# Prompt attention scores: the queries' lo parts multiplied with the 64 rows of the keys' hi, one component on each half of the rows

## The chip, the cores and the metric

The kernel runs on one core of one Trainium2 chip. The metric is device time in microseconds (us) of one execution, the median over runs. A core has a matrix engine (TensorE, PE in the profile; its weight loads are listed apart as PEld), a vector engine (VectorE, DVE), a scalar engine (ScalarE, ACT), GpSimd (POOL) and a queue engine that issues transfers (SyncE, SP). SBUF is the working memory with 128 rows (partitions); TensorE accumulates into PSUM.

## What is computed

One step of a decoder layer: a combined input projection, a state-space group, differential attention, an output projection and a gated feed-forward part with a short convolution. The change touches the prompt's attention scores only:

```python
def _scores(q, k):            # c: two components of 64 numbers per head
    return jnp.einsum('bthcd,bshcd->bhcts', q, k).astype(jnp.float32) * (QK_DIM ** -0.5)

def _diff_weights(s, lam):
    p = jax.nn.softmax(s, axis=-1)
    return p[:, :, 0] - lam * p[:, :, 1]

# bounds: 16 meta tokens, then blocks of 128 queries; L = 2064, 4 heads
for s0, e0 in bounds:
    s = _scores(q[:, s0:e0], k[:, :e0])
    mask = jnp.arange(e0)[None, :] <= jnp.arange(s0, e0)[:, None]
    w = _diff_weights(jnp.where(mask, s, NEG), lam)
    outs.append(jnp.einsum('bhts,bshe->bthe', w.astype(v.dtype), v[:, :e0]))
```

## The kernel before

Float32 products are made of two reduced-precision parts: a number x is split into hi (what the matrix engine's faster 32-bit format, fp32r, holds) and lo = x - hi.

**Where the parts come from.** `put_k` and `put_q` take one 128-token tile of the projection, normalise it per head, transpose it and split it. The keys go to scratch memory `KST[h, c]`, 128 rows deep: rows 0 to 63 the hi part of component c, rows 64 to 127 its lo part. The queries go to `QST[s, h, c]`, s = 0 for hi and 1 for lo, 64 rows each.

**The scores.** `attend` walks over two halves of the sequence, four heads in each, and in each of these over groups `g` of two 128-query tiles. `load_queries` fetches a group's queries into `qs` and writes each part twice, into rows 0 to 63 and into rows 64 to 127, so that one matmul over 128 rows multiplies one part of the query with hi and lo of the key. `attend_scores` makes one 128-query tile: for each component c, and for each piece z of at most 512 keys, a PSUM buffer `S` (a pool of four) gets qhi x (khi + klo) (L468), qlo x (khi + klo) (L469) and, where the piece touches the diagonal, a causal mask by a bfloat16 matmul (L472). DVE then takes the row maximum (L474) and ACT the exponential (L475), which frees the `S` buffer. After all pieces of a component come small steps that join the pieces (L480 to L484); after both components POOL and DVE form the weighted difference (L505, L507). `attend_values` transposes the weights (`tpw`, L530) and multiplies them with the values (`O`, L537).

**What sets the order.** The program is written tile by tile, but a scheduler in the compiler decides the order in which each engine's instructions stand, from priorities and its own estimate of times; an engine then runs its list in that order. While the attention runs, the scheduler puts matmuls of two later stages between it: the state-space half of the output projection (`out_ssm`, tile `po`, operands `sa`) and the first tiles of the attention half (`out_attention`, tile `po`, operands `oa`). These are written with `mm3` (L80, L81, L82: hi x hi, hi x lo, lo x hi). Later stages named below: `sample_attention` (tiles `tps`, `os`, `att`) and the feed-forward's up projection (tile `g`, again `mm3`).

Of the kernel before, what the change touches and what calls it, by code (L numbers as in the profile page):

```python
# [10 lines left out]
F32 = mybir.dt.float32  # L11
# [3 lines left out]
AF = mybir.ActivationFunctionType  # L15
ALU = mybir.AluOpType
AX = mybir.AxisListType
# [3 lines left out]
P = 128  # L21
D = 1024
KT = D // P
NM = 16
TP = 2064
# [35 lines left out]
class Step:  # L61
# [278 lines left out]
    def put_k(self, wp, pt, pj, t, n):  # L340
        nc, o = self.nc, self.o
        kg = self.heads_norm(wp, pj, n, self.gk)
        m = min(n, TP - t * P)
        kp = o["k_prompt"][0, 0].rearrange("t h d -> t (h d)")
        nc.sync.dma_start(out=kp[t * P : t * P + m], in_=kg[:m])
        if m < n:
            nc.sync.dma_start(out=o["k_sample"][0].rearrange("s t h d -> (s t) (h d)"), in_=kg[m:n])
        hi, lo = self.heads_T(wp, pt, kg, n, self.kTs)
        for c in range(2):
            for x, at in ((hi, 0), (lo, 64)):  # L350
                nc.sync.dma_start(
                    out=self.KST[:, c, at : at + 64, t * P : t * P + m].rearrange("h d t -> d h t"),
                    in_=x[c * 64 : c * 64 + 64, :, :m].bitcast(F32))
# [76 lines left out]
    def load_queries(self, qs, h, q0, q1):  # L430

        for dup in range(2):
            for s in range(2):
                self.nc.sync.dma_start(out=qs[dup * 64 : dup * 64 + 64, s, :, : q1 - q0].bitcast(F32),
                                       in_=self.QST[s, h, :, :, q0:q1].rearrange("c d t -> d c t"))

    def attend_queries(self, grp, wp):
        h, g = grp["h"], grp["g"]
# [6 lines left out]
    def attend_scores(self, grp, qi, wp, vp, ps):  # L445

        nc = self.nc
        qs, kt = grp["qs"], grp["head"]["kt"]
        M = P if qi else NM
        W = NM + P * qi  # L450
        Wall = NM + P * grp["nb"]
        qa = (NM + P * (qi - 1) if qi else 0) - grp["q0"]
        Z = P - NM
        diag = W - M
        nz = -(-W // 512)
        cuts = [W * z // nz // 2 * 2 for z in range(nz + 1)]
        pw, sums, fs = [], [], []
        for c in range(2):

            p = vp.tile([P, P - NM + TP], F32, name="p", tag="p", bufs=7)  # L460
            nms = wp.tile([P, 5], F32, name="nms", tag="nms", bufs=12)
            sms = wp.tile([P, 5], F32, name="sms", tag="sms", bufs=12)
            for z in range(nz):
                x, y = cuts[z], cuts[z + 1]
                S = ps.tile([P, 512], F32, name="S", tag="S", bufs=4)
                dst = S[:M, : y - x]
                masked = y > diag
                nc.tensor.matmul(dst, lhsT=qs[:, 0, c, qa : qa + M], rhs=kt[c][:, x:y], start=True, stop=False)  # L468
                nc.tensor.matmul(dst, lhsT=qs[:, 1, c, qa : qa + M], rhs=kt[c][:, x:y], start=False, stop=not masked)  # L469
                if masked:  # L470
                    lo_ = max(diag, x)
                    nc.tensor.matmul(dst[:, lo_ - x : y - x], lhsT=self.identB[:, :M],  # L472
                                     rhs=self.maskB[:, lo_ - diag : y - diag], start=False, stop=True)
                nc.vector.tensor_reduce(out=nms[:M, z : z + 1], in_=dst, axis=AX.X, op=ALU.max, negate=True)  # L474
                nc.scalar.activation(p[:M, Z + x : Z + y], dst, AF.Exp, bias=nms[:M, z : z + 1], accum_out=sms[:M, z : z + 1])  # L475
            sm, f = sms[:, 0:1], None
            if nz > 1:

                nm = wp.tile([P, 1], F32, name="nm", tag="nm", bufs=12)
                nc.vector.tensor_reduce(out=nm[:M], in_=nms[:M, :nz], axis=AX.X, op=ALU.min)  # L480
                f = wp.tile([P, 5], F32, name="f", tag="f", bufs=12)
                nc.scalar.activation(f[:M, :nz], nms[:M, :nz], AF.Exp, scale=-1.0, bias=nm[:M])
                sm = wp.tile([P, 1], F32, name="sm", tag="sm", bufs=12)
                nc.vector.scalar_tensor_tensor(out=sms[:M, :nz], in0=f[:M, :nz], scalar=1.0, in1=sms[:M, :nz],  # L484
                                               op0=ALU.mult, op1=ALU.mult, accum_out=sm[:M])
            pw.append(p)
            sums.append(sm)
            fs.append(f)

        cf = wp.tile([P, 1], F32, name="cf", tag="cf", bufs=8)  # L490
        c0 = wp.tile([P, 1], F32, name="c0", tag="c0", bufs=8)
        nc.vector.reciprocal(cf[:M], sums[1][:M])
        nc.gpsimd.tensor_tensor(out=c0[:M], in0=sums[0][:M], in1=self.nlam[:M], op=ALU.mult)
        nc.gpsimd.tensor_tensor(out=cf[:M], in0=cf[:M], in1=c0[:M], op=ALU.mult)
        w = pw[0]
        nc.gpsimd.memset(w[:M, 0:Z], 0.0)
        if nz == 1:
            nc.vector.scalar_tensor_tensor(out=w[:M, Z : Z + W], in0=pw[1][:M, Z : Z + W], scalar=cf[:M],
                                           in1=w[:M, Z : Z + W], op0=ALU.mult, op1=ALU.add)
        else:  # L500
            g = wp.tile([P, 5], F32, name="g", tag="gf", bufs=8)
            nc.gpsimd.tensor_tensor(out=g[:M, :nz], in0=fs[1][:M, :nz], in1=cf[:M].to_broadcast([M, nz]), op=ALU.mult)
            for z in range(nz):
                x = slice(Z + cuts[z], Z + cuts[z + 1])
                nc.gpsimd.tensor_tensor(out=pw[1][:M, x], in0=pw[1][:M, x],  # L505
                                        in1=g[:M, z : z + 1].to_broadcast([M, x.stop - x.start]), op=ALU.mult)
                nc.vector.scalar_tensor_tensor(out=w[:M, x], in0=w[:M, x], scalar=fs[0][:M, z : z + 1], in1=pw[1][:M, x],  # L507
                                               op0=ALU.mult, op1=ALU.add)
        if W < Wall:
            nc.gpsimd.memset(w[:M, Z + W : Z + Wall], 0.0)  # L510
        z = qi - 9 * grp["head"]["half"]
        nc.gpsimd.tensor_tensor(out=grp["head"]["e2"][:M, z : z + 1], in0=sums[0][:M], in1=sums[0][:M], op=ALU.mult)
        return w
# [1226 lines left out]
```

## Time and profile before

| | |
|---|---|
| median of 3 runs | 2938.07 us (2932.61 to 2941.27) |
| profiled execution | 2936.48 us, its span 2934.7 us |
| mean granted TensorE clock | 0.973 |
| PE busy | 2750.9 us (94%), 14916 matmuls |
| DVE / ACT / POOL busy | 2225.7 (76%) / 1403.3 (48%) / 1000.8 us (34%) |
| score matmuls | 360 at L468, 360 at L469, 136 masks at L472, from 642.8 us to 1186 us |

How to read it: a matmul's start is recorded, its end is modelled, and matmuls overlap in the pipeline, so the time that one costs is read from its start to the next one's start, not from its listed duration. A busy PE is therefore not a PE without waste; an idle PE has certainly waited. In the listings "128\*128 128x412" is a weight tile of 128 rows and 128 columns through which 412 columns pass; the number ahead of the star is the count of rows that take part. The granted clock is given as a share of 2.4 GHz; 0.5 would be the lower of the clock's two levels.

### The profile page before, as it was taken

How to read it: one execution, taken by the hardware profiler on the slowest of the kernel's cores; microseconds unless marked ns; L12 is line 12 of the kernel's file. 1: busy time of each engine (PE TensorE's matmuls, PEld its weight loads, DVE VectorE, ACT ScalarE, POOL GpSimd, SP SyncE). 2: the span in 40 equal slices, each digit the busy share in tenths (PEclk: the TensorE clock that was granted, in tenths of full speed). 3: DMA queues.
4: the chain of work that ended last, by engine and by line, in shares of the span. 5: the costliest groups of instructions: out<-in, count | busy, mean ns of one | idle time of the engine just before them, and what ended most of it. 6: DMA issues, size and time to landing. Idle time of an engine off the chain costs nothing.

```text
span 2934.7 us, 43647 instructions
## 1 busy us (share of the span) xinstructions
PE 2750.9 (94%) x14916; PEld 2364.0 (81%) x14916; DVE 2225.7 (76%) x4317; ACT 1403.3 (48%) x2859; POOL 1000.8 (34%) x1381
## 2 busy tenths in 40 slices
PE   6989989979999899787999999999999998999999
PEld 6966667867887777676998998988999997778776
DVE  6748876757678898557898878898889994675566
ACT  3323223545556666335566556665565562222234
POOL 4525442115445576564243432343214441000000
PEclk9999999989999999999999999999999999999999
DMA  7876776977864332587455546454454447676554
GB/s 224 255 194 149 205 216 168 236 216 195 230 182 141 116 113 83 166 266 228 156 161 186 160 145 213 145 181 159 133 168 130 127 125 290 216 245 195 178 190 132
DMA packets 452553, 529.73 MB, mean 181 GB/s; under 512 B 91546, under 2 KB 353578, under 8 KB 451305
## 3 DMA queue, kind: packets, MB, share of 16 engines
q1 hardware_dynamic: 360584, 385.75, 45.0%
q10 hardware_dynamic: 72848, 72.79, 7.5%
q0 software_dynamic: 18896, 68.39, 7.4%
q8 instruction: 118, 1.93, 0.3%
q14 instruction: 107, 0.87, 0.1%
HBM read 390.49 MB, written 135.14 MB: 179 GB/s over the span
## 4 chain that ended last, share of the span: by engine, by line
PE 55%; DVE 9%; DMA 8%; POOL 2%; issue 2%; ACT 2%; SPq 0%; ACTq 0%; POOLq 0%; DVEq 0%
PE g L80 8%; PE g L81 8%; PE g L82 8%; PE pq L80 4%; PE pq L81 4%; PE pq L82 4%; PE O L537 3%; DVE p L507 2%; DMA ot<-RR 2%; PE po L80 1%; DMA oraw<-in_w_out_dram 1%; DMA dt<-MT 1%; PE po L81 1%; PE po L82 1%; PE tps L632 1%
## 5 line engine op out<-in xcount | busy, mean ns | idle before, releaser
L80 PE MATMUL g<-xb,uw 128*128 128x384 f32 (+1 forms) x1848 | 594.0, 324 | 8.8 <-DVE A L1408 4.8
L81 PE MATMUL g<-xb,uw 128*128 128x384 f32 (+1 forms) x1848 | 595.8, 323 | 1.2 <-DVE xb L69 1.2
L82 PE MATMUL g<-xb,uw 128*128 128x384 f32 (+1 forms) x1848 | 584.7, 322 | 0.4 <-DVE uw L69 0.4
L80 PEld LDWEIGHTS g<-xb,uw 128*128 128x128 f32 x1848 | 346.8, 188 | 19.3 <-DVE A L1408 5.3
L81 PEld LDWEIGHTS g<-xb,uw 128*128 128x128 f32 x1848 | 347.9, 188 | 9.1 <-issue 2.3
L82 PEld LDWEIGHTS g<-xb,uw 128*128 128x128 f32 x1848 | 346.1, 188 | 7.0 <-issue 1.2
L475 ACT ACTIVATE p<-S,nms 128x484 f32<-128x484 f32 (+11 forms) x360 | 210.1, 589 | 157.6 <-DVE nms L474 136.0
L80 PE MATMUL pq<-dw,da 128*128 128x512 f32 x616 | 245.9, 401 | 19.6 <-ACT da L68 11.8
L69 DVE TENSOR_TENSOR uw<-uraw,uw 128x512 fp32r<-128x512 f32 x330 | 239.5, 734 | 26.7 <-ACT uw L68 24.7
L68 ACT ACTIVATE uw<-uraw 128x512 fp32r<-128x512 f32 x330 | 201.0, 625 | 114.6 <-PE g L82 77.2
L81 PE MATMUL pq<-dw,da 128*128 128x512 f32 x616 | 245.5, 399 | 0.0
L82 PE MATMUL pq<-dw,da 128*128 128x512 f32 x616 | 236.9, 398 | 0.0
L474 DVE TENSOR_REDUCE nms<-S 128x1 f32<-128x484 f32 (+11 forms) x360 | 190.9, 554 | 40.9 <-PE S L469 27.4
L68 ACT ACTIVATE da<-dt 128x1024 fp32r<-128x1024 f32 x66 | 69.8, 1058 | 249.4 <-PE pq L82 149.3
L95 POOL TENSOR_TENSOR rs_y<-rs_v,half 128x8 f32<-128x8 f32 (+4 forms) x77 | 105.8, 1377 | 243.9 <-DVE rs_v L90 225.9
L80 PE MATMUL pj<-wh,x 128*128 128x512 f32 (+1 forms) x408 | 170.6, 419 | 8.1 <-ACT wh L74 5.7
L81 PE MATMUL pj<-wl,x 128*128 128x512 f32 (+1 forms) x408 | 170.3, 417 | 2.7 <-DVE wl L75 2.6
L82 PE MATMUL pj<-wh,x 128*128 128x512 f32 (+1 forms) x408 | 169.6, 416 | 0.0
L468 PE MATMUL S<-kt,qs 128*128 128x484 f32 (+11 forms) x360 | 145.7, 407 | 23.3 <-ACT p L475 13.5
L1311 POOL TENSOR_TENSOR uraw<-uraw 128x512 f32<-128x512 f32 x66 | 108.0, 1637 | 160.6 <-DVE s L1309 112.4
L80 PEld LDWEIGHTS pq<-dw,da 128*128 128x128 f32 x616 | 117.2, 190 | 50.5 <-ACT da L68 12.7
L505 POOL TENSOR_TENSOR p<-p,g 128x412 f32<-128x412 f32 (+13 forms) x164 | 156.5, 983 | 3.4
(423 smaller groups left out, 6895.7 us busy)
## 6 DMA issues: line engine op xcount, KB each, us to landing
dt<-MT SPq DMA_DIRECT2D x99, 512.0 KB
uraw<-in_w_gate_dram SPq DMA_DIRECT2D x66, 512.0 KB
uraw<-in_w_up_dram SPq DMA_DIRECT2D x66, 512.0 KB
raw<-in_w_in_dram SPq DMA_DIRECT2D x80, 256.0 KB
MT<-z ACTq DMA_DIRECT2D x44, 384.0 KB
dT<-in_w_down_dram SPq DMA_DIRECT2D x66, 256.0 KB
qs<-QST SPq DMA_DIRECT2D x128, 128.0 KB
draw<-in_w_down_dram SPq DMA_DIRECT2D x55, 256.0 KB
```

Of the source, the lines that this page charges most:

```text
L68: nc.scalar.activation(hi, src, AF.Copy)
L69: nc.vector.tensor_tensor(out=lo, in0=src, in1=hi.bitcast(F32), op=ALU.subtract)
L80: mm(out, lhsT=lh, rhs=rh, start=start, stop=False, skip_group_check=goes_on)
L81: mm(out, lhsT=lh, rhs=rl, start=False, stop=False, skip_group_check=goes_on)
L82: mm(out, lhsT=ll, rhs=rh, start=False, stop=stop, skip_group_check=goes_on)
L95: nc.gpsimd.tensor_tensor(out=y, in0=v, in1=e, op=ALU.pow)
L468: nc.tensor.matmul(dst, lhsT=qs[:, 0, c, qa : qa + M], rhs=kt[c][:, x:y], start=True, stop=False)
L474: nc.vector.tensor_reduce(out=nms[:M, z : z + 1], in_=dst, axis=AX.X, op=ALU.max, negate=True)
L475: nc.scalar.activation(p[:M, Z + x : Z + y], dst, AF.Exp, bias=nms[:M, z : z + 1], accum_out=sms[:M, z : z + 1])
L505: nc.gpsimd.tensor_tensor(out=pw[1][:M, x], in0=pw[1][:M, x], in1=g[:M, z : z + 1].to_broadcast([M, x.stop - x.start]), op=ALU.mult)
L537: nc.tensor.matmul(O[:, :N], lhsT=v, rhs=tw[:, m - a, :N], start=(m == 0), stop=(m == nb))
L1311: gp.tensor_tensor(out=a21, in0=a11, in1=a21, op=ALU.subtract)
```

## The change

Three edits.

- `put_k`: for component 1 the halves of `KST` swap places, so that khi lies in rows 0 to 63 for component 0 and in rows 64 to 127 for component 1.
- `load_queries`: hi is still written twice for both components; of lo only component 0 goes to rows 0 to 63 and component 1 to rows 64 to 127. The number of transfers stays (144), half of them carry half the bytes.
- `attend_scores`: the loop over components moves inside the loop over pieces. For one piece both components get the 128-row pass with qhi and their mask; then come two matmuls with qlo that read 64 rows only, component 0 on rows 0 to 63, component 1 on rows 64 to 127; then maximum and exponential of both. The product qlo x klo is no longer formed.

```diff
         for c in range(2):
-            for x, at in ((hi, 0), (lo, 64)):
+
+            for x, at in ((hi, 64 * c), (lo, 64 - 64 * c)):
                 nc.sync.dma_start(
                     out=self.KST[:, c, at : at + 64, t * P : t * P + m].rearrange("h d t -> d h t"),
...
         for dup in range(2):
-            for s in range(2):
-                self.nc.sync.dma_start(out=qs[dup * 64 : dup * 64 + 64, s, :, : q1 - q0].bitcast(F32),
-                                       in_=self.QST[s, h, :, :, q0:q1].rearrange("c d t -> d c t"))
+            rows = slice(dup * 64, dup * 64 + 64)
+            self.nc.sync.dma_start(out=qs[rows, 0, :, : q1 - q0].bitcast(F32),
+                                   in_=self.QST[0, h, :, :, q0:q1].rearrange("c d t -> d c t"))
+            self.nc.sync.dma_start(out=qs[rows, 1, dup, : q1 - q0].bitcast(F32), in_=self.QST[1, h, dup, :, q0:q1])
...
-            for z in range(nz):
-                x, y = cuts[z], cuts[z + 1]
+        for z in range(nz):
+            x, y = cuts[z], cuts[z + 1]
+            masked = y > diag
+            dst = []
+            for c in range(2):
                 S = ps.tile([P, 512], F32, name="S", tag="S", bufs=4)
-                dst = S[:M, : y - x]
-                masked = y > diag
-                nc.tensor.matmul(dst, lhsT=qs[:, 0, c, qa : qa + M], rhs=kt[c][:, x:y], start=True, stop=False)
-                nc.tensor.matmul(dst, lhsT=qs[:, 1, c, qa : qa + M], rhs=kt[c][:, x:y], start=False, stop=not masked)
+                dst.append(S[:M, : y - x])
+                nc.tensor.matmul(dst[c], lhsT=qs[:, 0, c, qa : qa + M], rhs=kt[c][:, x:y], start=True, stop=False)
                 if masked:
                     lo_ = max(diag, x)
-                    nc.tensor.matmul(dst[:, lo_ - x : y - x], lhsT=self.identB[:, :M],
-                                     rhs=self.maskB[:, lo_ - diag : y - diag], start=False, stop=True)
-                nc.vector.tensor_reduce(out=nms[:M, z : z + 1], in_=dst, axis=AX.X, op=ALU.max, negate=True)
-                nc.scalar.activation(p[:M, Z + x : Z + y], dst, AF.Exp, bias=nms[:M, z : z + 1], accum_out=sms[:M, z : z + 1])
+                    nc.tensor.matmul(dst[c][:, lo_ - x : y - x], lhsT=self.identB[:, :M],
+                                     rhs=self.maskB[:, lo_ - diag : y - diag], start=False, stop=False)
+
+            for c in range(2):
+                r = slice(64 * c, 64 * c + 64)
+                nc.tensor.matmul(dst[c], lhsT=qs[r, 1, c, qa : qa + M], rhs=kt[c][r, x:y], start=False, stop=True)
+            for c in range(2):
+                p, nms, sms = stat[c]
+                nc.vector.tensor_reduce(out=nms[:M, z : z + 1], in_=dst[c], axis=AX.X, op=ALU.max, negate=True)
+                nc.scalar.activation(p[:M, Z + x : Z + y], dst[c], AF.Exp, bias=nms[:M, z : z + 1], accum_out=sms[:M, z : z + 1])
```

In the changed file the hi pass stands at L472, the mask at L475, the lo pass at L480, the transposes of the weights at L541 and the value matmuls at L548. The scheduler orders the new program again. PE's list, one head of the second half, a tile of 452-column pieces, before (the number behind a tile's name tells buffers apart; kt_9062 holds component 0 of the keys, kt_9064 component 1):

```order
L530 MATMUL tpw_9430<-ident_63,p_9163 128x128 x4
L530 MATMUL tpw_9441<-ident_63,p_9085 128x128 x4
L468 MATMUL S_9353<-kt_9062,qs_9262 128x452
L469 MATMUL S_9353<-kt_9062,qs_9262 128x452
L468 MATMUL S_9358<-kt_9062,qs_9262 128x452
L469 MATMUL S_9358<-kt_9062,qs_9262 128x452
L468 MATMUL S_9363<-kt_9062,qs_9262 128x452
L469 MATMUL S_9363<-kt_9062,qs_9262 128x452
L472 LDWEIGHTS identB_68
L472 MATMUL S_9363<-maskB_76,identB_68 128x128
L468 MATMUL S_9378<-kt_9064,qs_9262 128x452
L469 MATMUL S_9378<-kt_9064,qs_9262 128x452
```

The same tile's pieces in PE's list of the changed kernel:

```order
L472 MATMUL S_9361<-kt_9062,qs_9262 128x452
L480 MATMUL S_9361<-kt_9062,qs_9262 128x452
L541 MATMUL tpw_9447<-ident_63,p_9163 128x128 x3
L472 MATMUL S_9363<-kt_9064,qs_9262 128x452
L480 MATMUL S_9363<-kt_9064,qs_9262 128x452
L541 MATMUL tpw_9447<-ident_63,p_9163 128x128
L541 MATMUL tpw_9458<-ident_63,p_9085 128x128 x3
L472 MATMUL S_9371<-kt_9062,qs_9262 128x452
L480 MATMUL S_9371<-kt_9062,qs_9262 128x452
```

The components alternate now, but the lo pass of component 0 (L480, kt_9062) stands right behind its own hi pass, ahead of component 1's hi pass; the two lo passes of a piece are apart, with 128-row matmuls between them.

PE's list of the changed kernel at a piece with the diagonal, one head further on:

```order
L472 MATMUL S_11159<-kt_10875,qs_11118 128x420
L475 LDWEIGHTS identB_68
L475 MATMUL S_11159<-maskB_76,identB_68 128x128
L480 MATMUL S_11159<-kt_10875,qs_11118 128x420
L472 MATMUL S_11162<-kt_10877,qs_11118 128x420
L475 LDWEIGHTS identB_68
L475 MATMUL S_11162<-maskB_76,identB_68 128x128
L480 MATMUL S_11162<-kt_10877,qs_11118 128x420
L472 MATMUL S_11207<-kt_10875,qs_11118 128x452
```

Here the mask has moved from behind the lo pass to between the hi pass and the lo pass of its component; before, it was followed by another buffer's work.

## Rows read from the trace of the kernel before

**Rows 1.** The page's first part: busy time, share of the span, instructions

```profile
PE 2750.9 (94%) x14916; PEld 2364.0 (81%) x14916; DVE 2225.7 (76%) x4317; ACT 1403.3 (48%) x2859; POOL 1000.8 (34%) x1381
```

**Rows 2.** Busy us of each engine by stretch: start:end, length, engines, clock, DMA share, GB/s

```profile
640.00:700.00 60.00, 49.13 (x236) 37.84 (x237) 42.08 (x120) 34.59 (x111) 23.76 (x69) 0.85 0.87 244
700.00:900.00 200.00, 200.00 (x1103) 168.81 (x1101) 147.91 (x407) 104.95 (x350) 92.47 (x238) 0.98 0.67 190
900.00:1200.00 300.00, 276.54 (x1485) 224.69 (x1484) 262.03 (x625) 190.19 (x552) 180.43 (x293) 0.98 0.37 110
```

**Rows 3.** Chain of waits, its shares by line, 700 to 900 us, then 900 to 1200

```profile
by line: PE O L537 20.7%; PE po L80 13.5%; PE po L82 12.9%; PE po L81 12.8%; PE S L468 12.2%; PE tpw L530 10.9%; PE S L469 10.7%; PE SS L552 3.8%; PE S L472 2.4%; PE tpr L564 0.2%
...
by line: DVE p L507 16.4%; DVE nms L474 12.3%; PE O L537 9.7%; DMA ot<-RR 6.1%; POOL p L505 4.7%; issue 4.6%; PE tpw L530 3.7%; PE S L468 3.5%; DMA oraw<-in_w_out_dram 3.4%; DVE wT L534 3.2%; PE S L469 2.8%; DVE sms L484 2.6%; PE po L80 2.4
```

**Rows 4.** The lo pass L469 alone by stretch: PE, PEld, clock, DMA share, GB/s

```profile
640.00:700.00 60.00, 14.38 (x40) 8.86 (x40) 0.85 0.87 244
700.00:900.00 200.00, 42.15 (x128) 24.45 (x128) 0.98 0.67 190
900.00:1200.00 300.00, 69.36 (x193) 36.73 (x192) 0.98 0.37 110
```

**Rows 5.** PE's timeline in the scores: start us, listed duration, instruction

```profile
1023.82 0.37 PE L469 MATMUL S<-kt,qs 128*128 128x484 f32 x1
1024.04 0.23 PE L472 MATMUL S<-maskB,identB 128*128 128x128 bf16 x1
1024.08 0.47 PE L81 MATMUL po<-owl,oa 128*128 128x512 f32 x1
1024.39 0.35 PE L468 MATMUL S<-kt,qs 128*128 128x412 f32 x1
1024.58 0.35 PE L469 MATMUL S<-kt,qs 128*128 128x412 f32 x1
```

**Rows 6.** PE's timeline, a 32-row matmul between 128-row ones (sample attention)

```profile
1530.98 0.34 PE L82 MATMUL g<-xb,uw 128*128 128x384 f32 x1
1531.24 0.44 PE L680 MATMUL os<-vnh,swT 32*64 32x512 f32 x1
1531.62 0.44 PE L80 MATMUL g<-xb,uw 128*128 128x384 f32 x1
1531.90 0.33 PE L81 MATMUL g<-xb,uw 128*128 128x384 f32 x1
```

**Rows 7.** PEld's timeline at the same place, idle time before in brackets

```profile
1531.24 0.13 PEld L680 LDWEIGHTS os<-vnh,swT 32*64 32x64 f32 x1 [0.25 <-ACT vh L686]
1531.62 0.19 PEld L80 LDWEIGHTS g<-xb,uw 128*128 128x128 f32 x1 [0.24 <-issue]
```

**Rows 8.** PE's timeline, sixteen 64-row transposes between 128-row matmuls

```profile
1496.34 0.33 PE L82 MATMUL g<-xb,uw 128*128 128x384 f32 x1
1496.51 0.34 PE L81 MATMUL g<-xb,uw 128*128 128x384 f32 x1
1496.78 1.21 PE L672 MATMUL tps<-ident,Ss 64*128 64x64 f32 x16
1497.92 0.45 PE L82 MATMUL g<-xb,uw 128*128 128x384 f32 x1
1498.21 0.34 PE L80 MATMUL g<-xb,uw 128*128 128x384 f32 x1
```

**Rows 9.** PE's timeline, 64-row float32 matmuls, then 128-row ones of 512 columns

```profile
1538.73 0.34 PE L81 MATMUL g<-xb,uw 128*128 128x384 f32 x1
1539.00 1.04 PE L699 MATMUL att<-om,sel 64*32 64x512 f32 x2
1539.97 0.45 PE L680 MATMUL os<-vh,swT 128*64 128x512 f32 x1
1540.26 0.39 PE L681 MATMUL os<-vl,swT 128*64 128x512 f32 x1
1540.48 0.39 PE L680 MATMUL os<-vh,swT 128*64 128x512 f32 x1
```

More of the change, by code (lines that the diff above doesn't have):

```diff
@@ L457, in attend_scores @@
         pw, sums, fs = [], [], []
+        stat = []
         for c in range(2):
-            p = vp.tile([P, P - NM + TP], F32, name="p", tag="p", bufs=7)
-            nms = wp.tile([P, 5], F32, name="nms", tag="nms", bufs=12)
-            sms = wp.tile([P, 5], F32, name="sms", tag="sms", bufs=12)
-            for z in range(nz):
-                x, y = cuts[z], cuts[z + 1]
+            stat.append((vp.tile([P, P - NM + TP], F32, name="p", tag="p", bufs=7),
+                         wp.tile([P, 5], F32, name="nms", tag="nms", bufs=12), wp.tile([P, 5], F32, name="sms", tag="sms", bufs=12)))
@@ L476, in attend_scores @@
+        for c in range(2):
+            p, nms, sms = stat[c]
             sm, f = sms[:, 0:1], None
```

## The prediction

> **What bounds the kernel now.** The page's first part says which engine to suspect: TensorE is busy for 94% of the span, DVE for 76% [rows 1]. That is an average, so the table of busy times by stretch comes next, over the part in which scores are made [rows 2]. It shows three regimes. From 640 to 700 us TensorE is busy for 49.1 of 60 us: the stage starts and waits for its first data. From 700 to 900 us it is busy for all 200 us, DVE for 148: here TensorE alone is the limit. From 900 to 1200 us TensorE is idle for 300 - 276.5 = 23.5 us and DVE is busy for 262 of 300. The chain of waits agrees [rows 3]: from 700 to 900 us every line of it is TensorE's (the scores' two passes 12.2% and 10.7%), from 900 to 1200 us DVE's weighted difference and row maximum lead, and TensorE's lines follow. So time added to TensorE's list is paid whole between 700 and 900 us, and after 900 us once its 23.5 us of waiting are used up.
>
> **Costs of a matmul, from starts to next starts.** A lo pass of 484 columns takes 0.22 us, a hi pass of 412 columns 0.19 us [rows 5]. The cost goes with the columns; nothing in these rows lets fewer rows make it shorter. The question is what it costs to stand a 64-row matmul among 128-row ones. Before, the scores use 128 rows throughout; other stages have such neighbours.
>
> The nearest row in kind is a 32-row matmul of the same number format, alone between 128-row ones [rows 6]. From the start of the 128-row matmul ahead of it (1530.98) to the second start behind it (1531.90) pass 0.92 us. Undisturbed the three would take 0.17 + 0.22 + 0.17 = 0.56 us (384 columns 0.17 in rows 8, 512 columns 0.22 in rows 9). So going in and out costs about **0.35 us**: 0.09 ahead of it, 0.16 in it, 0.11 behind it. The weight loads show why [rows 7]: both PEld rows stand behind 0.25 and 0.24 us of idle, so in neither case were the weights loaded while the matmul ahead was running.
>
> With 64 rows the same edges are there: at the transposes 1496.51 to 1496.78 is 0.27 instead of 0.17, and 1497.92 to 1498.21 is 0.29 instead of 0.17, together 0.22 us [rows 8]; at the float32 matmuls 0.27 instead of 0.17 and 0.29 instead of 0.22, together **0.17 us** [rows 9]. What these lose inside can't be told apart from their own work, so 0.17 is the lower end. I take 0.35, the row that has the format of the new matmuls and its cost in full; its edges (0.09 and 0.11) are those of the 64-row rows.
>
> The Trainium skill has a rule for this: "TensorEngine Tiling (Array Packing)", section Key Properties, says that changing the tiling mode, and not just the tile, drains the engine. That speaks against this change, and rows 6 and 7 agree with 0.35 us for a way in and out.
>
> **Part 1, the lo pass on 64 rows.** It removes no columns: 360 lo matmuls before, 360 after, of the same widths. What decides is how they stand in TensorE's list. The text of the change puts the two components' lo matmuls side by side; the scheduler does not. In the order shown above the lo pass of component 0 follows its own hi pass, and 128-row matmuls stand between the two lo passes of a piece. Counted over the whole list, the 360 lo matmuls form 341 runs: 323 of one, 17 of two, one of three. Only 18 of 180 pairs touch. So there are **341 ways in and out**: 341 x 0.35 = 119 us of TensorE time.
>
> **Part 2, the masks.** Before, 93 of the 136 masks are followed by a matmul of the fp32r format (a hi pass or `po`), and that one takes 0.31 instead of 0.22 us, for its weights come late (1024.08 to 1024.39, rows 5). After, 134 masks stand between hi and lo of their own buffer, where the lo pass waits anyway. That gives back up to 93 x 0.09 = 8 us. Sum on TensorE: 119 - 8 = 111 us.
>
> **Part 3, what costs nothing.** DVE's, ACT's and POOL's instructions are the same in number and size. Half of the query transfers carry half the bytes; the DMA engines are busy for 37% to 67% of the time after 700 us [rows 2], so smaller transfers free nothing that was short. The swapped halves of the keys' scratch move nothing in time. The two components now end together, so their joining steps bunch up; the work on other tiles covers it, and if that cover fails it can cost at most the idle time that I count as used up below (23.5 us).
>
> **Where the 111 us land.** The lo passes lie 40, 128 and 193 to the three stretches [rows 4], so 11%, 35% and 54%: 12, 39 and 60 us. From 640 to 700 us there are 10.9 us of idle time; between 0 and 12 us, I take 6. From 700 to 900 us nothing hides it: 39. From 900 to 1200 us the waiting of 23.5 us goes first: 60 - 23.5 = 36. Sum: 6 + 39 + 36 = **81 us**. On the profiled execution's 2936.5 us that is 3017.5; the median of the runs is 1.6 us above that execution, so 3019 us. Behind the stage nothing gives the time back: the same `po` matmuls stand inside it before and after, 552 of them.
>
> Ends: with 0.17 us for a run the sum is 341 x 0.17 - 8 = 50 us, of which the first stretch's 6 vanish, 17 are paid and 27 - 23.5 = 4 remain: 21 us, 2959 us. With 0.35 and no idle time used up, because the waits after 900 us stay as long as they are, all 111 us are paid: 3049 us.
>
> **Rivals.**
> *A. The 64-row fp32r matmul costs nothing extra*, the loss in rows 6 being one of 32 rows, that in rows 8 and 9 one of other formats. Then only the masks' 8 us remain, half of them in the stretch with waiting: about 2930 to 2934 us, no change that can be told (0.3%, 8.8 us, is about what a measurement of this kernel can tell). Against it: three kinds of matmul show the same edges. It decides from a price of 0.1 us for a run: 341 x 0.1 - 8 = 26 us, of which 9 are paid between 700 and 900 us and the rest lies in idle time. Chance 0.07.
> *B. The pairs run at the same time*, which ends on the other side. Two matmuls on different halves of the rows would take the time of one, 0.19 us less for a pair, 34 us for 180 pairs, if they touched. They touch at 18 places: 3 us. With A's price that is 2938 - 8 - 3 = 2927 us, just faster. No row before shows two matmuls side by side in different rows. Chance 0.03. (The Trainium skill, "TensorE: Matmul & The Clock Gate", Part 3 on row and column tiling, has them start about 4 ns apart; by it a pair would save what is said here, but only where it touches, and no run here shows it yet.)
> *C. The clock falls.* TensorE's granted clock is 0.98 from 700 us on and was 0.85 in the stretch in which it waits most [rows 2]. If the new gaps bring the 500 us behind to 0.85 as well, streaming grows by 0.98/0.85 - 1 = 15%, at most 76 us more: up to 3095 us. Against it: behind the edges of rows 9 the second matmul passes 512 columns in 0.22 us, which is the higher level of the clock (2.4 GHz), and no row shows an edge that brings it down. Chance 0.05.
>
> **How the numbers follow.** The forecast has 0.85, A 0.07, B 0.03, C 0.05. Predicted is 3019 us; the range is the forecast's own, 2959 to 3049, which leaves out A, B and C, 0.15 in all. Slower by over 0.3%: 0.85 + 0.05 = 0.90. Within 0.3%: 0.07. Faster: 0.03.
>
> **What would show it.** In the profile after, from a 128-row matmul's start to the start of the lo pass behind it some 0.09 us more than its columns take, the lo pass itself 0.16 more, the next one 0.11 more; PEld idle ahead of almost every lo pass's weights and ahead of the next. The stretch of the scores longer by some 80 us, with TensorE's waits for ACT and DVE in it shorter, and everything behind it shifted and not longer. Wrong: a lo pass that starts without a gap (A); two that start within a few ns, at many places (B); a granted clock under 0.95 in the scores (C); the added time lying behind the scores, which would mean that the scheduler's new order costs something I did not see.

## The result: slower by 3.2%, close to the forecast

| | before | changed |
|---|---|---|
| median of the runs beside each other | 2939.67 us | 3034.82 us |
| ratio | | 1.0322, 95% interval 1.0298 to 1.0347 |
| span of the profiled execution | 2934.7 us | 3030.0 us |

The forecast was 81 us more (3019 us, range 2959 to 3049); it became 95 us more.

Where the time lies is read from the same views as before. First the page's first part of the changed kernel (busy us, share, instructions); it answers to [rows 1]:

```profile
PE 2860.4 (94%) x14916; PEld 2378.9 (79%) x14916; DVE 2220.8 (73%) x4317; ACT 1411.3 (47%) x2859; POOL 994.5 (33%) x1381
```

The same number of matmuls, 110 us more of TensorE. The table by stretch (start:end, length, PE, PEld, DVE, ACT, POOL, granted clock, DMA share, GB/s), against [rows 2]:

```profile
640.00:700.00 60.00, 52.11 (x181) 33.72 (x182) 34.69 (x98) 30.62 (x91) 20.24 (x57) 0.72 0.73 208
700.00:900.00 200.00, 200.00 (x920) 145.72 (x918) 117.39 (x348) 92.96 (x304) 72.35 (x209) 0.97 0.53 159
900.00:1200.00 300.00, 299.05 (x1328) 205.90 (x1328) 227.07 (x527) 166.96 (x479) 146.66 (x255) 0.99 0.35 105
```

In the 200 us in which TensorE was the limit it now makes 920 matmuls instead of 1103. From 900 to 1200 us it is idle for 1 us instead of 23.5: the stretch in which DVE led has become TensorE's as well. The chain of waits, shares by line, 700 to 900 us and 900 to 1200 us, says the same against [rows 3]; the lo pass (L480) has 17.3% and 21.2% of it, before (L469) 10.7% and 2.8%:

```profile
by line: PE O L548 19.3%; PE S L480 17.3%; PE po L80 13.5%; PE S L472 12.5%; PE po L82 11.2%; PE po L81 10.6%; PE tpw L541 10.2%; PE SS L563 2.8%; PE S L475 2.3%; PE tpr L575 0.2%
...
by line: PE O L548 23.5%; PE S L480 21.2%; PE S L472 16.0%; PE tpw L541 13.1%; PE po L80 6.6%; PE po L82 6.3%; PE po L81 6.3%; PE SS L563 1.6%; DMA oraw<-in_w_out_dram 1.2%; PE S L475 1.1%; PE tp L179 1.0%; issue 0.6%; DVE nms L483 0.4%; DV
```

The cost of one lo pass can be read from TensorE's timeline of the changed kernel (start us, listed duration, instruction):

```profile
865.94 0.40 PE L81 MATMUL po<-owl,sa 128*128 128x512 f32 x1
866.18 0.39 PE L82 MATMUL po<-owh,sa 128*128 128x512 f32 x1
866.41 0.38 PE L472 MATMUL S<-kt,qs 128*128 128x484 f32 x1
866.72 0.48 PE L480 MATMUL S<-kt,qs 64*128 64x484 f32 x1
867.12 0.50 PE L80 MATMUL po<-owh,sa 128*128 128x512 f32 x1
867.46 0.39 PE L81 MATMUL po<-owl,sa 128*128 128x512 f32 x1
867.69 0.38 PE L472 MATMUL S<-kt,qs 128*128 128x484 f32 x1
```

From each start to the next one: the hi pass ahead of the lo pass takes 0.31 us where 484 columns take 0.22 [rows 5], 0.09 more; the lo pass 0.40, 0.18 more; the matmul behind it 0.34 where 512 columns take 0.23 (867.46 to 867.69), 0.11 more. Together 0.38 us at this place. Over the whole trace a lone lo pass takes 0.21 us more than its columns would at 2.4 GHz (median of 321 without idle time behind them), in the kernel before 0.02 us more (median of 339). The weight loads at the same place show that neither the lo pass's weights nor those behind it are loaded ahead (idle time before in brackets), as in [rows 7]:

```profile
866.18 0.19 PEld L472 LDWEIGHTS S<-kt,qs 128*128 128x128 f32 x1
866.71 0.18 PEld L480 LDWEIGHTS S<-kt,qs 64*128 64x128 f32 x1 [0.35 <-issue]
867.12 0.19 PEld L80 LDWEIGHTS po<-owh,sa 128*128 128x128 f32 x1 [0.23 <-issue]
867.23 0.19 PEld L81 LDWEIGHTS po<-owl,sa 128*128 128x128 f32 x1
```

Scores and value products began at 642.8 us and ended at 1212 us before; in the changed kernel they run from 644.9 to 1297 us. So 83 of the 95 us are in that stage, 2 us ahead of it, 10 us behind it, as the two profiled executions have it.

### The profile page after: what moved, and what is told of

The parts are those of the page before. It is cut to its first block, busy times and chain, and to the rows that moved or that the text cites. A ratio compares the mean times of both kernels' runs of the same rounds, so it can differ in the third digit from the quotient of the medians.

```text
span 3030.0 us, 43593 instructions
## 1 busy us (share of the span) xinstructions
PE 2860.4 (94%) x14916; PEld 2378.9 (79%) x14916; DVE 2220.8 (73%) x4317; ACT 1411.3 (47%) x2859; POOL 994.5 (33%) x1381
## 4 chain that ended last, share of the span: by engine, by line
PE 60%; DVE 8%; DMA 6%; issue 2%; POOL 2%; ACT 1%; SPq 0%; ACTq 0%; POOLq 0%; DVEq 0%
PE g L82 7%; PE g L80 7%; PE g L81 7%; PE O L548 5%; PE S L480 4%; PE pq L80 4%; PE pq L81 4%; PE pq L82 4%; PE S L472 3%; PE tpw L541 2%; DVE uw L69 2%; PE po L80 2%; PE po L82 2%; PE po L81 2%; PE tps L643 1%
## 5 line engine op out<-in xcount | busy, mean ns | idle before, releaser
L483 DVE TENSOR_REDUCE nms<-S 128x1 f32<-128x484 f32 (+11 forms) x360 | 197.2, 561 | 110.3 <-PE S L480 107.3
L472 PE MATMUL S<-kt,qs 128*128 128x484 f32 (+11 forms) x360 | 153.6, 434 | 9.2 <-DMA qs<-QST 7.0
L480 PE MATMUL S<-kt,qs 64*128 64x484 f32 (+11 forms) x360 | 155.5, 456 | 0.0
```

What stands on the lines that cost most here:

```text
L472: nc.tensor.matmul(dst[c], lhsT=qs[:, 0, c, qa : qa + M], rhs=kt[c][:, x:y], start=True, stop=False)
L480: nc.tensor.matmul(dst[c], lhsT=qs[r, 1, c, qa : qa + M], rhs=kt[c][r, x:y], start=False, stop=True)
L483: nc.vector.tensor_reduce(out=nms[:M, z : z + 1], in_=dst[c], axis=AX.X, op=ALU.max, negate=True)
```

## The experiments

The theory (H): a 64-row matmul among 128-row ones costs about 0.4 us for the way in and out, and the scheduler leaves 341 such ways. The rival (O): the new order, with the components interleaved and their joining steps late, is what costs. A second question was whether the pairs would pay if they really stood back to back.

The times below are medians, and the kernel before has been run beside each group of experiments. Its executions spread over 27 us (2919.69 to 2946.38 in the first group). The recorded ratios of the experiments with four executions stand on a base 4 to 10 us above the median of all the executions of the kernel before (3035.40 / 1.0322 = 2941 against 2932), so differences of 10 us between experiments carry no argument here.

**The order alone.** The changed kernel's loops, lo pass on 128 rows:

```diff
-                r = slice(64 * c, 64 * c + 64)
-                nc.tensor.matmul(dst[c], lhsT=qs[r, 1, c, qa : qa + M], rhs=kt[c][r, x:y], start=False, stop=True)
+                nc.tensor.matmul(dst[c], lhsT=qs[:, 1, c, qa : qa + M], rhs=kt[c][:, x:y], start=False, stop=True)
```

with the old `put_k` and `load_queries`. 

> The changed kernel's loops, but the lo pass reads all 128 rows as before, with the old layout of the keys and the old loads of the queries; the lo product of both lo parts is formed again. Theory H (the way in and out of a 64-row matmul costs 0.40 us, 341 times): no 64-row matmul is left among the scores, so the time falls back to the kernel before, 2930 to 2950 us; the lo pass is listed as 128*128 and starts without a gap. Rival O (the new order of the components, with their joining steps bunched at the end of a tile, starves the engines): most of the 95 us stays, 3010 to 3035 us.

Measured: 2922.76 us against 2932.03 us of the kernel before, ratio 0.9968 (0.9946 to 0.9991). That is under the 2930 to 2950 us that H gave. The rival falls: the order costs nothing, it is 9 us better. Against these loops the 64 rows cost 3034.8 - 2922.8 = 112 us; taken against the kernel before that ran beside each of them it is 95 + 9 = 104 us. The order alone also goes back to the old layout and the old loads; in the changed kernel TensorE waits for neither, since it has 1 us of idle time from 700 to 1200 us. The table of the order alone from 900 to 1200 us looks like that of before, TensorE waiting for 23 us again:

```profile
900.00:1200.00 300.00, 277.20 (x1503) 226.41 (x1501) 259.86 (x611) 182.24 (x534) 183.47 (x291) 0.99 0.40 120
```

**The rows alone.** The loops of the kernel before, lo pass on 64 rows, new layout and loads:

```diff
-                nc.tensor.matmul(dst, lhsT=qs[:, 1, c, qa : qa + M], rhs=kt[c][:, x:y], start=False, stop=not masked)
+                r = slice(64 * c, 64 * c + 64)
+                nc.tensor.matmul(dst, lhsT=qs[r, 1, c, qa : qa + M], rhs=kt[c][r, x:y], start=False, stop=not masked)
```

> The loops of the kernel before, but the lo pass reads 64 rows, with the new layout of the keys and the new loads. Its list has 359 runs of lo matmuls instead of 341. Theory H: 359 x 0.40 = 144 us on TensorE, less some 25 to 37 us of idle time that is used up: 3040 to 3065 us, slower than the changed kernel. Rival O: within 15 us of the kernel before, 2925 to 2955 us.

Measured: 3035.40 us, ratio 1.0322 (1.0287 to 1.0357). Far from the rival's 2955 us; 5 us under the lower end of what H gave, so the 18 more ways in and out than in the changed kernel do not show. Nor is it a comparison of the ways alone, for the granted clock is 0.96 here where the changed kernel has 0.99. TensorE has no idle time left from 900 to 1200 us:

```profile
900.00:1200.00 300.00, 300.00 (x1293) 202.76 (x1294) 223.88 (x522) 163.97 (x469) 138.88 (x247) 0.96 0.34 101
```

**Half of the heads.** The changed kernel, heads 2 and 3 with 128-row lo passes:

```diff
-                r = slice(64 * c, 64 * c + 64)
+                r = slice(64 * c, 64 * c + 64) if grp["h"] < 2 else slice(0, P)
```

with lo of both components loaded into all rows for these heads. 

> The changed kernel, but heads 2 and 3 load both components' lo into all 128 rows and make the lo pass on 128 rows; heads 0 and 1 keep the 64-row lo pass. About 171 runs of 64-row matmuls are left of 341. Theory H (a price for each way in and out): 171 x 0.40 = 68 us on TensorE above the same loops without 64-row matmuls (2923 us), less the idle time that goes first: 2960 to 2985 us, about half of the way to the changed kernel. A rival by which the first few 64-row matmuls already cost most of it (a lasting effect such as a lower clock): 3010 us or more.

Measured: 2975.68 us against 2933.92 us, ratio 1.0129 (1.0096 to 1.0162). That is 53 us above the loops without 64-row matmuls (2922.76 us, from another group of runs), 47% of the whole 112 us with half of the ways (171): about half, as H said, and not the 3010 us of a lasting effect. Of the 23 us of idle time from 900 to 1200 us, 8.4 us are left:

```profile
900.00:1200.00 300.00, 291.59 (x1472) 222.24 (x1471) 254.38 (x598) 185.42 (x541) 170.42 (x282) 1.00 0.36 111
```

**Pairs that really touch, and their control.** The changed kernel with both components' scores in one PSUM tile of two banks, so that both hi passes get their buffer at once:

```diff
+            S = ps.tile([P, 2, 512], F32, name="S", tag="S", bufs=2)
             for c in range(2):
-                S = ps.tile([P, 512], F32, name="S", tag="S", bufs=4)
-                dst.append(S[:M, : y - x])
+                dst.append(S[:M, c, : y - x])
```

TensorE's list then has 177 runs of two lo matmuls. The control is the same with 128-row lo passes. 

> The changed kernel, but both components' scores lie in one PSUM tile of two banks (two such tiles instead of four single ones), so that the two hi passes can start together; in TensorE's list 177 of 180 pairs of lo matmuls then stand side by side and there are 181 runs. Theory H with overlap inside a pair: 181 x 0.40 = 72 us, less 178 x 0.17 = 30 us that the second matmul of a pair no longer takes: 42 us above its control with 128-row lo passes, and at most that above the kernel before if the control equals it, 2960 to 2990 us. If the two matmuls of a pair do not overlap: 72 us above the control. A rival in which back to back is all that was missing: at or below the control.

> The control to the paired kernel: the same two-bank tiles and the same order, the lo pass on 128 rows with the old layout and loads. Theory H: no 64-row matmul among the scores, so within 20 us of the kernel before, a little slower if the coarser PSUM tiles make TensorE wait longer for ACT: 2935 to 2960 us. Rival O: 3010 us or more, since the components are interleaved here too.

Measured: the pairs 2990.02 us, ratio 1.0164 (1.0128 to 1.0201); the control 2977.01 us, ratio 1.0129 (1.0096 to 1.0161). Two of the numbers were missed. The control is 45 us above the kernel before (38 us by the ratio), not 20 at most, and 54 us above the order alone, which has the same loops with four single banks. TensorE is idle for 38 us from 900 to 1200 us (300 - 262.15), and its waits for ACT ahead of a score grow from 5.0 us in the order alone to 23.6 us:

```profile
900.00:1200.00 300.00, 262.15 (x1350) 216.56 (x1349) 250.22 (x556) 180.45 (x507) 163.78 (x270) 0.93 0.36 108
```

And the pairs are only 13 us above the control, not 42; the two intervals overlap a little. In the profiled executions the stage, from the first score to the last value product, grows from 611 to 629 us, while TensorE's idle time in it falls from 61 to 50 us: of some 28 us more on TensorE 10 lie in what had been idle time, and those 28 us are themselves under the 42. The timelines show what a touching pair does. The paired kernel:

```profile
850.01 0.69 PE L472 MATMUL S<-kt,qs 128*128 128x484 f32 x2
850.62 0.48 PE L480 MATMUL S<-kt,qs 64*128 64x484 f32 x2
851.04 0.70 PE L548 MATMUL O<-wT,v 128*128 128x256 f32 x2
851.57 0.38 PE L548 MATMUL O<-wT,vt 128*128 128x256 f32 x1
```

Its control, at the same piece:

```profile
850.30 0.69 PE L471 MATMUL S<-kt,qs 128*128 128x484 f32 x2
850.82 0.60 PE L478 MATMUL S<-kt,qs 128*128 128x484 f32 x2
851.26 0.59 PE L546 MATMUL O<-wT,v 128*128 128x256 f32 x2
851.69 1.46 PE L546 MATMUL O<-wT,vt 128*128 128x256 f32 x6
```

The two 64-row lo passes together are listed with 0.48 us, as long as one alone in the changed kernel (866.72 above): they run at the same time. Over the whole trace their starts lie 3 to 4 ns apart (median of 179). From the first hi pass to the value product they take 1.03 us, the control 0.96, and the two value products behind take 0.53 instead of 0.43: 0.17 us more in all. So even a pair that overlaps fully does not win back the edges: what it saves is one pass of 0.22 us, what it pays is 0.22 + 0.17, some 0.39.

**Pairs on the same rows.** The paired kernel, both components in rows 0 to 63 (old layout of the keys, lo loaded there for both):

```diff
-                r = slice(64 * c, 64 * c + 64)
+                r = slice(0, 64)
```

> The paired kernel (two-bank score tiles, lo pairs back to back), but both components' lo passes read rows 0 to 63: the keys' old layout, lo loaded into rows 0 to 63 only. Theory H with overlap by different rows: the second matmul of a pair now has to wait for the first; 180 pairs x 0.17 = 31 us more on TensorE than with different halves, of which up to half may lie in TensorE's idle time: 3003 to 3022 us. The two starts of a pair lie about 0.17 us apart instead of some 4 ns. Rival (back to back is what counts, not the halves): as the paired kernel with different halves, 2980 to 2997 us.

Measured: 3016.46 us against 2933.92 us, ratio 1.0267 (1.0233 to 1.0301), 26 us above the pairs on different halves. TensorE's timeline at a pair:

```profile
855.33 0.69 PE L474 MATMUL S<-kt,qs 128*128 128x484 f32 x2
855.95 0.70 PE L482 MATMUL S<-kt,qs 64*128 64x484 f32 x2
856.59 0.28 PE L577 MATMUL tpr<-ident,rs_y 128*9 128x128 f32 x1
```

The pair takes 0.64 us (855.95 to 856.59) instead of 0.42. So it is the different halves that let two matmuls run at once, and not that they stand side by side. The starts lie 0.295 us apart (median of 180), more than the 0.17 us of the columns that I expected.

**The mask's place.** The kernel before, only with the mask between hi and lo:

```diff
-                nc.tensor.matmul(dst, lhsT=qs[:, 1, c, qa : qa + M], rhs=kt[c][:, x:y], start=False, stop=not masked)
                 if masked:
                     lo_ = max(diag, x)
                     nc.tensor.matmul(dst[:, lo_ - x : y - x], lhsT=self.identB[:, :M],
-                                     rhs=self.maskB[:, lo_ - diag : y - diag], start=False, stop=True)
+                                     rhs=self.maskB[:, lo_ - diag : y - diag], start=False, stop=False)
+                nc.tensor.matmul(dst, lhsT=qs[:, 1, c, qa : qa + M], rhs=kt[c][:, x:y], start=False, stop=True)
```

> The kernel before with one edit: the mask stands between the hi and the lo pass (128 rows), as in the changed kernel. The weights of the matmul behind a mask come 0.09 us late either way; before, 93 of 136 masks had such a matmul behind them, here all 136 have. If the mask's place is what makes the changed kernel's loops with 128-row lo passes 9 us faster than the kernel before: 2922 to 2928 us. If it isn't: up to 43 x 0.09 = 4 us slower or the same, 2930 to 2938 us, and the gain is that of the interleaved components.

Measured: 2924.86 us, ratio 0.9970 (0.9953 to 0.9987): the same 9 us as the order alone. So moving the mask, with the order that the scheduler makes of it, is enough for a gain of this size, and that interleaving the components adds to it is not shown. Why it gains stays open. The late weights behind a mask are still there (the lo pass behind a mask takes 0.10 us more than its columns at 2.4 GHz in this kernel, median of 126; one that is not, 0.02 us), so it is not the term that I had priced. The profiled execution reaches its first score at 631.5 us instead of 642.8 us, behind a transfer:

```profile
631.50 1.10 PE L468 MATMUL S<-kt,qs 128*128 128x456 f32 x2 [7.68 <-DMA qs<-QST]
632.39 0.33 PE L471 MATMUL S<-maskB,identB 128*128 128x128 bf16 x1
```

That is 11 us ahead of the scores, before the mask could do anything itself. In the profiled execution of the order alone the scores begin 5 us earlier than before, and 16 us are won inside the stage, where this kernel wins 4; so the two gains need not have one cause. One profile each does not say whether it is so in every execution. Both this kernel and the order alone are faster than the kernel before and the changed one; neither has a 64-row lo pass.

## Why the prediction was right, step by step

- **TensorE is the limit, wholly from 700 to 900 us and after 900 us once 23.5 us are used up.** Right: 200 of 200 us, and 1 us of idle time left from 900 to 1200.
- **341 ways in and out, since the scheduler parts the pairs.** Right, and it is the step that decided the size. It did not decide the sign: in the paired kernel 181 ways were left, and the 64 rows still cost 13 us above the control.
- **0.35 us for each.** Right in mechanism and in size. At the place shown it is 0.09 ahead, 0.18 in, 0.11 behind, 0.38 us. The 32-row row [rows 6] was the right one to take; the edges alone, 0.17 us and my lower end, leave out the time lost between the lo pass's start and the next one, which is the largest part. Over the stage the tables of the order alone, of before and of the changed kernel give the price:

```profile
640.00:1190.00 550.00, 524.08 (x2869) 433.88 (x2868) 456.65 (x1158) 329.77 (x1015) 294.02 (x601) 0.99 0.52 154
640.00:1212.00 572.00, 536.39 (x2875) 439.56 (x2875) 455.42 (x1158) 332.30 (x1015) 299.07 (x601) 0.97 0.53 153
640.00:1297.00 657.00, 644.32 (x2873) 453.18 (x2874) 453.78 (x1158) 341.34 (x1016) 291.87 (x601) 0.96 0.42 126
```

  TensorE is busy for 120 us more than in the order alone (118 us with the 2.5 us of scores that lie ahead of 640 us there), 0.35 us for each of 341 ways. Part of it may be the clock. If TensorE had work all the time, a granted clock of 0.96 takes 0.04 x 657 = 26 us of the stage, one of 0.99 takes 0.01 x 550 = 6 us; without these 20 us, an upper estimate, a way would cost 0.29 us.
- **8 us back from the masks.** Not shown. Where a mask stands ahead of the lo pass, the edge moves to the mask and is no smaller: in the changed kernel mask to lo is 0.16 us, lo to the next 0.39 for 432 columns, and that next one 0.34:

```profile
1273.49 0.36 PE L472 MATMUL S<-kt,qs 128*128 128x432 f32 x1
1273.69 0.23 PE L475 MATMUL S<-maskB,identB 128*128 128x128 bf16 x1
1273.85 0.46 PE L480 MATMUL S<-kt,qs 64*128 64x432 f32 x1
1274.24 0.51 PE L82 MATMUL po<-owh,oa 128*128 128x512 f32 x1
1274.58 0.59 PE L548 MATMUL O<-wT,vt 128*128 128x256 f32 x2
```

  A gain of 9 us did come with the new loops, and the mask's place with the order that follows gave as much alone, in a way that the runs did not settle.
- **Where it lands: 6 + 39 + 36.** The stage grew by 83 us, where 81 were forecast. On TensorE 108 us came (644.3 - 536.4) where 111 were forecast, and some 23 us of idle time were used up (572 - 536.4 before, 657 - 644.3 now) where 29.5 were. That the sum fits so closely is in part luck: 119 us for the ways stand against 120 in the control, but the 8 us that it takes off for the masks are not shown, and up to 9 of the 108 us may be the clock (0.96 of 657 us against 0.97 of 572).
- **Nothing behind the stage.** Not so: 10 us lie behind it and 2 ahead, which is most of the 14 us by which the forecast was short. The kernel's later order differs there. The time behind the stage is 1723 us before and 1732 in the changed kernel, but 1720 with the mask moved and 1742 with half of the heads, so it does not follow the number of 64-row matmuls; its cause stays open.
- **Rivals.** A fell at the rows 866.41 to 867.46. B's mechanism is real, 3 to 4 ns between the starts of a pair, but in the changed kernel it had 18 places, and at 177 it still did not pay. C fell as the main cause: the clock is 0.97 and 0.99 where it was 0.98. But from 640 to 700 us it is 0.72 where it was 0.85, and over the stage 0.96 where it was 0.97, the part named above. In the kernels with two-bank tiles, where TensorE waits longest, it is 0.93 to 0.94 from 900 to 1200 us.

## What to carry to other kernels

Half-empty rows of the matrix engine are no free time: a matmul on half of the rows was no shorter here, and each way from full rows to half rows and back cost 0.35 us over the stage (0.38 at the place shown), more than one and a half passes of 484 columns. Two half-row matmuls on different halves do run at once, but a pair saves one pass and pays one way in and out, so at these widths it loses. Longer runs in half-row form would share one way among more matmuls; no run here tried them. And read the order that the scheduler made, not the order in which the loops are written: "back to back" in the text was so at 18 of 180 places. With both scores in one buffer it was so at 177, so a wait for a second buffer between the two was enough to part them.

## What the runs showed of the hardware that I had not expected

- The largest part of the price lies between the half-row matmul's start and the next matmul's (0.18 of 0.38 us), not in the gap ahead of it. The next weights are loaded only at the end of that time (867.12).
- Two 64-row matmuls on different halves start 3 to 4 ns apart; on the same half 0.295 us apart, 0.1 us or more beyond their columns. The Trainium skill, "TensorE: Matmul & The Clock Gate", Part 3, gives about 4 ns for tiles in different row groups; the paired kernel's trace agrees.
- A two-bank PSUM tile in two buffers, in place of four single banks, cost 54 us with the order that the scheduler makes of it (2977 against 2923 us, the order alone). In this kernel the two halves come free only together; that this is the whole reason is not shown, for the granted clock from 900 to 1200 us is 0.93 there against 0.99.
